# V of both mixers in rows of tokens, with V groups and gates between mixer A's q-and-k jobs

## The chip, the cores and the metric

The kernel runs on one core of a Trainium2 chip. The core's engines each work through their own instructions in order: PE (TensorE) multiplies matrices and transposes, DVE (VectorE), ACT (ScalarE) and POOL (GpSimd) work on elements, and SP issues transfers between the core's memory and the chip's. PE's sums and transposes land in eight banks of PSUM, from where DVE or ACT takes them; a bank can be used again when what stood in it has been read. The metric is the device time of one execution in microseconds (us). Before the change it is 1679.69 us, the median of three runs (1675.78 to 1680.08).

## The reference

One layer for 1024 tokens of a prompt and 32 new ones (1056 in all), model width 1024. All projections read the normed input; mixer A picks keys by an index score and a top-k, mixer B is stick-breaking attention; both have 8 heads of 64.

```
def project_inputs(x, pos, g_mix, w_in, g_qn, g_kn):
    h = rmsnorm(x, g_mix)
    z = jnp.einsum('bld,de->ble', h, w_in)
    q_a, k_a, v_a, q_i, k_i, w_i, q_b, k_b, v_b, gate_a, gate_b = jnp.split(z, SPLIT_OFFSETS, axis=-1)
    q_a = rope(rmsnorm(q_a.reshape(B, L, N_HEADS_A, HEAD_DIM), g_qn), pos)
    k_a = rope(rmsnorm(k_a.reshape(B, L, N_HEADS_A, HEAD_DIM), g_kn), pos)
    v_a = v_a.reshape(B, L, N_HEADS_A, HEAD_DIM)
    ...
    v_b = v_b.reshape(B, L, N_HEADS_B, HEAD_DIM)
...
    h = x + W_out( sigmoid(g_A) * (o_A @ W_bA) + sigmoid(g_B) * (o_B @ W_bB) )
    y = h + W_down( relu(W_up rmsnorm(h))^2 )
```

The change concerns `v_a` and `v_b`, both 1056 x 512: they are outputs of the layer, and the attention reads them again.

## The kernel before, in words

The tokens are nine tiles: 0 to 7 of 128, and tile 8, `NEW`, of 32. The model width is eight blocks k of 128. Every fp32 matrix is held as a high part and a low part (`xh`, `xl` of the input; `wh`, `wl` of the weights), and each product is three matmuls: high x high, high x low, low x high.

`unit` loads 128 x 512 weights into `wst` (three places), lets ACT cast the high part `wh`, and lets POOL (later in the kernel also DVE) subtract to get `wl`; five places (`WB`) hold `wh` and `wl`. `early` calls `unit` ahead of a job. Two kinds of jobs use the units:

- `column_block`: 128 columns of weights stand still in PE, tokens move past in chunks of 512, 272 and 272, and the sum has the output's columns in its partitions. Gates, q and k of mixer B and V use it.
- `token_rows`: a tile of 128 tokens stands still and the weights move, so the sum has tokens in its partitions. q and k of mixer A use it (256 columns a job). For `NEW`, the high and low part stand still together in 64 rows, and `join` adds the lower 32 rows to the upper by a copy on ACT and an add on DVE.

`project_v` of before is a `column_block` of two units for each of four pairs of heads (p): DVE scales the sum into `vt`, `vt` goes out as a row block of a transposed V, PE transposes it tile by tile into banks `t`, ACT casts the high part into `vs`, DVE subtracts the low part, and both go to `dv` for the attention.

The stages around the change, in the order of `run`: index scores; `project_b` for p = 0 to 3 (q and k of B, then V of B for the same p); `top_k_begin` and `top_k`, a search of 31 halvings for the top-k bound, whose counting passes (`junk`) run on ACT and DVE beside PE, followed by pieces per tile (`sgn`, `sq`, `pen`, `pre`, `mask`) that settle ties; two gates; `rope_tables`; `project_a` for p = 0 to 3 (V of A for that p, then q and k of A in nine tiles, here qk0 to qk3); two gates; then the attention reads q, k and v back. In `project_a` a tile's sum is squared by ACT (`sq`), summed (`ss`), multiplied by the tables (`ta`, `tb`) on DVE and added on POOL into `qk`; after nine tiles come the factors, the scaling of k, the transposes of `qk` into banks `t`, and the split into `az`, which goes to `dq` and `dk`. `sq`, `ta` and `tb` have one place each.

No line of the kernel is run in the order in which it is written: a recording planner (class `Plan`) takes all instructions with their rank and puts each engine's in an order by ranks and estimated times, before the program is built. The lower rank goes first: FAST 0 (emptying of a bank), PREP 1 (units), MAIN 2 (all that isn't given another, `token_rows` among it), FILL 3 (`column_block`), SLOW 4 (the search). On the chip each engine keeps that order. The banks: two `pj`, three `s`, two `t`, one `o`.

All engine instructions are issued by one helper, so the profile shows them all as line 440 (441 in the changed kernel); they are told apart by the names of their tiles.

Of the kernel before, what the change touches and what calls it, by code (L numbers as in the profile page):

```python
# [22 lines left out]
KB = D // 128  # L23
# [27 lines left out]
PACE = 16  # L51
PA_BANKS = ('s', 'pj', 's', 's', 'pj')
# [407 lines left out]
class Layer:  # L460
# [103 lines left out]
    def run(self):  # L564
# [74 lines left out]
        for p in range(2, 4):  # L639
            self.project_b(p)  # L640
            with nc.behind():
                old, new = a["ck" + "ba"[p - 2]], self.dc[H * (3 - p):H * (4 - p)]
                nc.sync.dma_start(*(z.rearrange("j e t -> (j e) t") for z in (new, old)))
        with nc.rank(SLOW):
            self.top_k_begin()
        gates = iter([*range(KB, 2 * KB), *range(KB)])
        for _ in range(2):
            self.gate(next(gates), "zb")
        self.early(*(a["w_va"][0, j] for j in range(2)), *(a["w_qka"][0, j] for j in range(3)))
# [3 lines left out]
        for p in range(4):  # L653
            self.project_a(p)
        with nc.rank(SLOW):
            self.top_k()
        for _ in range(GATES_BEFORE - 2):
            self.gate(next(gates))
# [435 lines left out]
    def project_v(self, p, mixer, w, vout):  # L1094

        nc, pr = self.nc, self.pr
        units = [self.unit(w[p, j]) for j in range(2)]
        vt = nc.tile(pr, [128, T], F32, "vt", bufs=1)

        def done(c, cs, ps):  # L1100
            nc.vector.tensor_mul(vt[:, cs], ps, self.rb[:, cs])

        self.column_block(units, self.x_of, done, self.parts)
        nc.sync.dma_start(vout[p * 128:p * 128 + 128], vt)
        for sl in GROUPS:
            pt = self.bank("t")
            m = rows(sl[0])
            nt = len(sl)
            for i, s in enumerate(sl):
                nc.tensor.transpose(pt[:m, i * 128:i * 128 + 128], vt[:, 128 * s:128 * s + m], self.ident)  # L1110
            vs = nc.tile(pr, [128, 2, 4, 128], F32R, "vs", bufs=1)
            pv = pt.rearrange("p (t h e) -> p h t e", t=4, h=2)
            for h in range(2):
                vh = vs[:m, h, :nt, 0:HD]
                nc.scalar.copy(vh, pv[:m, h, :nt])
                nc.vector.tensor_sub(vs[:m, h, :nt, HD:], pv[:m, h, :nt], vh.bitcast(F32))
            for h in range(2):
                nc.sync.dma_start(self.dv[mixer * H + 2 * p + h, :m, sl[0]:sl[0] + nt], vs.bitcast(F32)[:m, h, :nt])
# [804 lines left out]
```

## Time and profile before

| what | value |
| --- | --- |
| median of three runs | 1679.69 us |
| profiled execution, its own time | 1679.89 us |
| its span, first to last instruction | 1678.1 us |
| V of mixer B on PE, p = 0 / 1 / 2 / 3, from | 104 / 160 / 201 / 237 us |
| gates ahead of mixer A, from | 249 us |
| q-and-k jobs qk0 / qk1 / qk2 / qk3, from | 272 / 312 / 353 / 395 us |
| gates behind, first matmul of the attention | 433, 468 us |
| counting passes of the top-k search | 176 to 340 us |

The span is what the profile covers; 1.8 us of the execution lie around it. The starts are those of the first matmul of each job in PE's timeline. "PE busy" counts matmuls from start to modelled end, and they overlap; so the rate of PE is read from the distance between starts.

### The profile page before, as it was taken

How to read it: one execution, taken by the hardware profiler on the slowest of the kernel's cores; microseconds unless marked ns; L12 is line 12 of the kernel's file. 1: busy time of each engine (PE TensorE's matmuls, PEld its weight loads, DVE VectorE, ACT ScalarE, POOL GpSimd, SP SyncE). 2: the span in 40 equal slices, each digit the busy share in tenths (PEclk: the TensorE clock that was granted, in tenths of full speed). 3: DMA queues.
4: the chain of work that ended last, by engine and by line, in shares of the span. 5: the costliest groups of instructions: out<-in, count | busy, mean ns of one | idle time of the engine just before them, and what ended most of it. 6: DMA issues, size and time to landing. Idle time of an engine off the chain costs nothing.

```text
span 1678.1 us, 34748 instructions
## 1 busy us (share of the span) xinstructions
PE 1663.3 (99%) x12244; PEld 1587.8 (95%) x12244; DVE 1355.1 (81%) x2830; ACT 945.1 (56%) x2008; POOL 804.2 (48%) x681
## 2 busy tenths in 40 slices
PE   9999999999999999999999999999999999999999
PEld 9898999899989999998989999999999999999999
DVE  6777899987579889887877649998988997678775
ACT  7556888764366768886665545333333453443431
POOL 4532332344356576354556348544433466345564
PEclk9999999999999999999999999999999999999999
DMA  8243454355573636788764644444444596676674
GB/s 284 61 125 107 142 185 144 99 155 148 163 218 103 181 100 178 190 264 247 227 188 142 178 123 134 157 146 142 142 142 135 198 326 223 204 232 200 222 227 137
DMA packets 182126, 290.31 MB, mean 173 GB/s; under 512 B 29472, under 2 KB 61696, under 8 KB 181920
## 3 DMA queue, kind: packets, MB, share of 16 engines
q1 hardware_dynamic: 181664, 287.91, 55.1%
q8 instruction: 97, 1.59, 0.4%
q14 instruction: 77, 0.63, 0.1%
q10 hardware_dynamic: 288, 0.17, 0.0%
HBM read 195.09 MB, written 94.90 MB: 173 GB/s over the span
## 4 chain that ended last, share of the span: by engine, by line
PE 84%; DVE 7%; DMA 4%; ACT 2%; issue 2%; POOL 1%; SPq 1%; DVEq 0%; ACTq 0%; POOLq 0%
PE pj L440 34%; PE c L440 11%; PE a L440 11%; PE b L440 11%; PE s L440 9%; PE o L440 4%; PE t L440 4%; DVE junk L440 2%; DMA xt<-x 1%; SPq L440 1%; DVE qi L440 0%; DVE y L440 0%; DMA q<-dq 0%; DMA kl<-dc 0%; DVE ta L440 0%
## 5 line engine op out<-in xcount | busy, mean ns | idle before, releaser
L440 PE MATMUL pj<-xl,wh 128*128 128x272 f32 (+2 forms) x1200 | 334.0, 312 | 0.0
L440 POOL TENSOR_TENSOR wl<-wst,wh 128x512 fp32r<-128x512 f32 x125 | 175.4, 1408 | 219.4 <-ACT wh L440 192.9
L440 PE MATMUL pj<-xh,wh 128*128 128x272 f32 (+1 forms) x768 | 251.7, 328 | 0.0
L440 PE MATMUL pj<-xh,wl 128*128 128x272 f32 (+1 forms) x768 | 250.6, 326 | 0.2 <-POOL wl L440 0.2
L440 PEld LDWEIGHTS pj<-xl,wh 128*128 128x128 f32 x1200 | 212.7, 188 | 10.0
L440 ACT CAST wh<-wst 128x512 fp32r<-128x512 f32 x197 | 120.7, 619 | 126.6 <-PE pj L440 35.0
L440 PEld LDWEIGHTS pj<-xh,wl 128*128 128x128 f32 x768 | 144.6, 188 | 10.8 <-POOL wl L440 0.5
L440 PEld LDWEIGHTS pj<-xh,wh 128*128 128x128 f32 x768 | 144.6, 188 | 10.1 <-DVE gz L440 0.3
L440 POOL TENSOR_TENSOR p<-p,rem 128x383 f32<-128x383 f32 (+8 forms) x66 | 107.2, 1639 | 64.7 <-DVE rem L440 31.1
L440 ACT CAST wh<-us 128x512 fp32r<-128x512 f32 x80 | 49.7, 621 | 122.6 <-PE pj L440 34.3
L440 DVE TENSOR_TENSOR tt<-t,tt 128x512 fp32r<-128x512 f32 (+2 forms) x168 | 100.2, 620 | 16.8 <-ACT tt L440 16.0
L440 DVE TENSOR_TENSOR_SCAN rem<-rem,first 128x384 f32<-128x384 f32 (+8 forms) x66 | 107.2, 1642 | 2.0 <-ACT rem L440 1.6
L440 POOL TENSOR_TENSOR wl<-y,wh 128x512 fp32r<-128x512 f32 x46 | 68.6, 1492 | 77.7 <-ACT wh L440 74.7
L440 ACT ACTIVATE junk<-score,cand 128x1024 bf16<-128x1024 f32 (+2 forms) x93 | 96.9, 1042 | 12.5 <-DVE cand L440 11.0
L440 ACT CAST wh<-y 128x512 fp32r<-128x512 f32 x79 | 49.0, 621 | 96.8 <-PE c L440 20.5
L440 ACT CAST tt<-t 128x512 fp32r<-128x512 f32 (+2 forms) x168 | 85.8, 540 | 27.5 <-PE t L440 18.5
L440 PE MATMUL o<-tt,v 128*128 128x256 f32 (+1 forms) x640 | 98.5, 279 | 0.5 <-DVE o L440 0.5
L440 PE MATMUL s<-k,q 128*128 128x512 f32 (+4 forms) x384 | 98.2, 351 | 0.7 <-DMA q<-dq 0.7
L440 PEld LDWEIGHTS o<-tt,v 128*128 128x128 f32 x640 | 90.5, 189 | 6.1 <-DVE o L440 1.1
L440 DVE TENSOR_SCALAR_CACHE_REDUCE junk<-score,cand 128x384 bf16<-128x384 f32 (+1 forms) x124 | 92.9, 749 | 3.1
L440 PE MATMUL t<-ident,p 128*128 128x128 f32 (+1 forms) x596 | 90.7, 275 | 0.0
L440 POOL TENSOR_SCALAR p<-p,nb 128x384 f32<-128x384 f32 (+6 forms) x66 | 53.5, 817 | 70.8 <-DVE nb L440 59.6
(401 smaller groups left out, 5624.3 us busy)
## 6 DMA issues: line engine op xcount, KB each, us to landing
us<-w_down SPq DMA_DIRECT2D x80, 256.0 KB, 3.3
q<-dq SPq DMA_DIRECT2D x64, 256.0 KB, 4.1
du<-us SPq DMA_DIRECT2D x56, 264.0 KB, 2.7
du<-y SPq DMA_DIRECT2D x56, 264.0 KB, 3.0
y<-w_up SPq DMA_DIRECT2D x44, 256.0 KB, 2.8
k<-dk SPq DMA_DIRECT2D x40, 256.0 KB, 4.1
v<-dv SPq DMA_DIRECT2D x40, 256.0 KB, 4.0
xl<-du SPq DMA_DIRECT2D x35, 264.0 KB, 4.7
```

What stands on the lines that cost most here:

```text
L440: fn(*args, **kw)
```

## The change

- **V in rows of tokens.** `project_v` now lets a tile of tokens stand still and moves 512 columns of weights, all eight heads, past it. It works in two groups (tiles 0 to 3, tiles 4 to 8), each of which goes through all eight blocks k and holds one bank for each tile (`V_BANKS`: pj, s, pj, s, s). Each group loads its eight units anew: 16 for each mixer where there were 8. A sum is emptied by ACT, which scales it into `vz` (two places), ACT casts `vs` (two places), DVE or POOL, whichever the planner finds free, subtracts, and `vz` goes out as rows of V, `vs` to `dv`. The transposes, `vt` and the multiplication by `rb` are gone. The matmuls keep rank FILL.
- **Places.** V of B stands once, behind all four `project_b`. One gate precedes mixer A. Group 0 of V of A comes ahead of qk0, group 1 ahead of qk1, a gate ahead of qk2 and of qk3, and one gate last.
- **More places.** `qk` has two, `az` four. `early` loads five units of V of A.
- On the host the layout of `w_va`, `w_vb` is changed, and the V outputs need no transposition.

```diff
+V_BANKS = ('pj', 's', 'pj', 's', 's')
...
+        self.project_v(1, a["w_vb"], self.o["v_b"])
         with nc.rank(SLOW):
             self.top_k_begin()
         gates = iter([*range(KB, 2 * KB), *range(KB)])
-        for _ in range(2):
-            self.gate(next(gates), "zb")
-        self.early(*(a["w_va"][0, j] for j in range(2)), *(a["w_qka"][0, j] for j in range(3)))
+        self.gate(next(gates), "zb")
+        self.early(*(a["w_va"][k] for k in range(WB)))
         nc.close(self.pr, self.ik)
         self.pr = nc.open("proja")
         self.rope_tables()
         for p in range(4):
+            if p < 2:
+                self.project_v(0, a["w_va"], self.o["v_a"], (p,))
+            else:
+                self.gate(next(gates))
             self.project_a(p)
+        for _ in range(GATES_BEFORE - 3):
+            self.gate(next(gates))
         with nc.rank(SLOW):
             self.top_k()
-        for _ in range(GATES_BEFORE - 2):
-            self.gate(next(gates))
...
-    def project_v(self, p, mixer, w, vout):
+    def project_v(self, mixer, w, vout, groups=(0, 1)):
...
+        mm = nc.tensor.matmul
+        for tiles in (SUMS[g] for g in groups):
+            banks = [self.bank(V_BANKS[i]) for i in range(len(tiles))]
+            for k in range(KB):
+                wh, wl = self.unit(w[k])
+                with nc.rank(FILL):
+                    for s, ps in zip(tiles, banks):
+                        first, last = k == 0, k == KB - 1
+                        if s == NEW:
+                            x = self.xh[1][:, k, SEQ - W1:]
+                            mm(ps[:2 * DEC], x, wh, start=first, stop=False)
+                            mm(ps[:2 * DEC], x, wl, start=False, stop=last)
+                            continue
+                        xh, xl = self.x_of(k, slice(128 * s, 128 * s + 128))
+                        mm(ps, xh, wh, start=first, stop=False)
+                        mm(ps, xh, wl, start=False, stop=False)
+                        mm(ps, xl, wh, start=False, stop=last)
+            for s, ps in zip(tiles, banks):
+                m = rows(s)
+                with nc.rank(FAST):
+                    if s == NEW:
+                        self.join(ps, nc.tile(pr, [128, 512], F32, "vz", bufs=2)[:DEC])
+                    z = nc.tile(pr, [128, 512], F32, "vz", bufs=2)
+                    nc.scalar.activation(z[:m], ps[:m], AF.Copy, scale=self.rs[:m, s:s + 1])
+                    vs = nc.tile(pr, [128, H, 128], F32R, "vs", bufs=2)
+                    zv = z.rearrange("p (h e) -> p h e", h=H)
+                    nc.scalar.copy(vs[:m, :, 0:HD], zv[:m])
+                nc.either.tensor_sub(vs[:m, :, HD:], zv[:m], vs.bitcast(F32)[:m, :, 0:HD])
+                nc.sync.dma_start(vout[128 * s:128 * s + m], z[:m])
+                nc.sync.dma_start(
+                    self.dv[mixer * H:mixer * H + H, :m, s].rearrange("g p e -> p g e"), vs.bitcast(F32)[:m])
...
-        self.project_v(p, 1, a["w_vb"], self.o["v_b"])
...
-        self.project_v(p, 0, a["w_va"], self.o["v_a"])
...
-        qk = nc.tile(pr, [128, NT, 4, HD], F32, "qk", bufs=1)
+        qk = nc.tile(pr, [128, NT, 4, HD], F32, "qk", bufs=2)
...
-                zz = nc.tile(pr, [128, 2, 512], F32R, "az", bufs=2)
+                zz = nc.tile(pr, [128, 2, 512], F32R, "az", bufs=4)
```

How the planner's order moves, at three places. **PE in qk1.** Before, tiles 0 to 3 of qk1 (banks s_3930, pj_3934, s_3938, s_3942) begin beside the end of a V column block, with a transpose of the job before (qk) and four of V (vt) between their matmuls:

```order
L440 MATMUL pj_3934<-wh3_3926,xh0_104 128x256
L440 MATMUL s_3938<-wh3_3926,xh0_104 128x256
L440 MATMUL s_3942<-wh3_3926,xh0_104 128x256
L440 MATMUL t_3898<-ident_91,qk_3845 128x32
L440 MATMUL pj_3946<-wh0_3917,xh1_106 128x256
L440 MATMUL s_3930<-wl3_3927,xh0_104 128x256
L440 MATMUL s_3930<-wh3_3926,xl0_105 128x256
L440 MATMUL s_3930<-wh3_3926,xh0_104 128x256
L440 MATMUL s_3930<-wl3_3927,xh0_104 128x256
L440 MATMUL s_3930<-wh3_3926,xl0_105 128x256
L440 MATMUL t_3910<-ident_91,vt_3906 128x128 x4
```

Now tile 7 of qk1 ends (s_3729), three transposes of qk follow, then the last matmul of V's group 1, tile NEW (s_3651), and tile 3 of qk1 (s_3713), which is given the same bank:

```order
L441 MATMUL s_3729<-wh1_3697,xh1_106 128x256
L441 MATMUL s_3729<-wl1_3698,xh1_106 128x256
L441 MATMUL s_3729<-wh1_3697,xl1_107 128x256
L441 MATMUL t_3742<-ident_91,qk_3699 128x128 x3
L441 MATMUL s_3651<-wl2_3675,xh1_106 64x512
L441 MATMUL s_3713<-wh3_3688,xh0_104 128x256
L441 MATMUL s_3713<-wl3_3689,xh0_104 128x256
L441 MATMUL s_3713<-wh3_3688,xl0_105 128x256
L441 MATMUL s_3713<-wh3_3688,xh0_104 128x256
L441 MATMUL s_3713<-wl3_3689,xh0_104 128x256
```

What moved: tile 3 of qk1 stands behind the last piece of V, with no other matmul between the two users of the bank.

**DVE at the same time**, at the end of the search. Before, the first tie piece (pre_4157, for tile 2 of the masks) stands among the tables and sums of qk1's tiles:

```order
L440 ISA pen_4153,lowa_4152<-pen_4153,score7_1273 128x1024
L440 ISA lowa_4152 128x1
L440 TENSOR_REDUCE ss_3929<-sq_3943 128x4
L440 TENSOR_TENSOR ta_3944<-s_3942,tabc_3827 128x256
L440 TENSOR_TENSOR tb_3945<-s_3942,tabs_3828 128x256
L440 SCALAR_TENSOR_TENSOR pre_4157<-sq_4156,minus_4149 128x384
L440 TENSOR_REDUCE ss_3929<-sq_3947 128x4
L440 TENSOR_SCALAR needa_4154<-pre_4157,cnta1_1467 128x1
L440 TENSOR_SCALAR tfb_4167<-small_1463 128x3
L440 SCALAR_TENSOR_TENSOR pre_4157<-pre_4157,needa_4154,sgn_4155 128x384
L440 TENSOR_TENSOR ta_3948<-pj_3946,tabc_3827 128x256
L440 TENSOR_TENSOR vs_3913<-t_3912,vs_3913 128x4x64 x2
```

Now the add that `join` needs for V's tile NEW (s_3651) stands behind the pieces pen and pre of the search:

```order
L441 TENSOR_SCALAR pen_3928<-score7_1241,tfa_3926 128x1024
L441 ISA pen_3928,lowa_3927<-pen_3928,score7_1241 128x1024
L441 ISA lowa_3927 128x1
L441 TENSOR_TENSOR small_1475<-cntb0_1482,small_1475 128x3
L441 COPY_PREDICATED small_1475<-small_1475,cand_1766 128x3
L441 TENSOR_SCALAR tfb_3942<-small_1475 128x3
L441 COPY lowb_3943<-tfb_3942 32x1
L441 SCALAR_TENSOR_TENSOR pre_3932<-sq_3931,minus_3924 128x384
L441 TENSOR_SCALAR needa_3929<-pre_3932,cnta1_1479 128x1
L441 SCALAR_TENSOR_TENSOR pre_3932<-pre_3932,needa_3929,sgn_3930 128x384
L441 TENSOR_TENSOR s_3651<-s_3651,vz_3684 32x512
L441 TENSOR_TENSOR vs_3686<-vz_3685,vs_3686 32x8x64
```

What moved: an instruction that empties the bank for qk1's tile 3 comes directly behind the first tie piece, with the tables of that tile (ta_3715) only after the next one.

**PE between the two V groups of mixer B.** Before, V of B is a column block for each p (here p = 3), whose transposes (vt) stand among the block's own matmuls:

```order
L440 MATMUL pj_1455<-xh1_106,wl2_1452 128x272
L440 MATMUL pj_1455<-xh1_106,wh2_1451 128x272
L440 MATMUL pj_1455<-xl1_107,wh2_1451 128x272
L440 MATMUL t_1457<-ident_91,vt_1453 128x128 x4
L440 MATMUL pj_1455<-xh1_106,wl2_1452 128x272
L440 MATMUL pj_1455<-xh1_106,wh2_1451 128x272
L440 MATMUL pj_1455<-xl1_107,wh2_1451 128x272
```

Now the last block k of group 0 (banks pj_1399 to s_1402) is followed at once by the first of group 1, whose bank pj_1435 is that of pj_1399 and s_1438 that of s_1400:

```order
L441 MATMUL pj_1401<-wh2_1425,xl0_105 128x512
L441 MATMUL s_1402<-wh2_1425,xh0_104 128x512
L441 MATMUL s_1402<-wl2_1426,xh0_104 128x512
L441 MATMUL s_1402<-wh2_1425,xl0_105 128x512
L441 MATMUL s_1436<-wh3_1441,xh1_106 128x512
L441 MATMUL pj_1435<-wh3_1441,xh1_106 128x512
L441 MATMUL pj_1435<-wl3_1442,xh1_106 128x512
L441 MATMUL pj_1435<-wh3_1441,xl1_107 128x512
L441 MATMUL s_1436<-wl3_1442,xh1_106 128x512
L441 MATMUL s_1436<-wh3_1441,xl1_107 128x512
L441 MATMUL s_1438<-wh3_1441,xh1_106 128x512
L441 MATMUL s_1438<-wl3_1442,xh1_106 128x512
```

What moved: four banks end within twelve matmuls, and the next group begins on the free bank s_1436 and on that of pj_1399.

More of the change, by code (lines that the diff above doesn't have):

```diff
@@ L1092, in rope_tables @@
                 S.rearrange("p t (s e) -> p t s e", s=2), gx)
-    def project_v(self, p, mixer, w, vout):
+    def project_v(self, mixer, w, vout, groups=(0, 1)):
         nc, pr = self.nc, self.pr
[L1097 to L1118, printed above, removed]
@@ L1859, in _host_arrays @@
         qi[:, 256:].reshape(4, 2, 128, NI_B).transpose(0, 2, 1, 3).reshape(4, 128, 512))
-    out["w_qb"], out["w_kb"], out["w_vb"], out["w_va"] = units(qb), units(kb), units(vb), units(va)
+    out["w_qb"], out["w_kb"] = units(qb), units(kb)
+    out["w_vb"], out["w_va"] = (np.ascontiguousarray(z).reshape(KB, 128, 512) for z in (vb, va))
     out["w_g"] = units(np.concatenate([ga, gb], axis=1))
@@ L1887, in _host_arrays @@
     return out
-_OUTS = {"yT": (128, KB, T), "k_a": (T, 512), "v_a": (512, T), "k_idx": (T, HD), "k_b": (512, T), "v_b": (512, T)}
+_OUTS = {"yT": (128, KB, T), "k_a": (T, 512), "v_a": (T, 512), "k_idx": (T, HD), "k_b": (512, T), "v_b": (T, 512)}
 def _build(nc, arrays):
@@ L1917 @@
     kap, kas = pair(r["k_a"].reshape(T, H, HD))
-    vap, vas = pair(np.ascontiguousarray(r["v_a"].T).reshape(T, H, HD))
+    vap, vas = pair(r["v_a"].reshape(T, H, HD))
     kip, kis = pair(r["k_idx"])
     kbp, kbs = pair(np.ascontiguousarray(r["k_b"].T).reshape(T, H, HD))
-    vbp, vbs = pair(np.ascontiguousarray(r["v_b"].T).reshape(T, H, HD))
+    vbp, vbs = pair(r["v_b"].reshape(T, H, HD))
     return tuple(np.ascontiguousarray(z) for z in (yp, ys, kap, vap, kip, kbp, vbp, kas, vas, kis, kbs, vbs))
```

## The prediction

> **What bounds the kernel now.** I read the page first: its busy shares, its slices, its chain.
>
> ```profile
> span 1678.1 us, 34748 instructions
> PE 1663.3 (99%) x12244; PEld 1587.8 (95%) x12244; DVE 1355.1 (81%) x2830; ACT 945.1 (56%) x2008; POOL 804.2 (48%) x681
> PE 84%; DVE 7%; DMA 4%; ACT 2%; issue 2%; POOL 1%; SPq 1%; DVEq 0%; ACTq 0%; POOLq 0%
> ```
>
> TensorE (PE) is busy 99% of the span and makes 84% of the chain. So the time is what PE has to stream, plus its gaps. The change lies between about 104 us (V of mixer B) and 474 us (start of attention), so next come stretches of it: from and to, length, then busy time and instructions of PE, of its weight loads, of DVE, ACT and POOL, the clock granted, DMA.
>
> ```profile
> 82.00:200.00 118.00, 118.00 (x722) 106.25 (x723) 89.48 (x200) 78.61 (x169) 34.26 (x36) 1.00 0.41 118
> 200.00:280.00 80.00, 80.00 (x520) 73.43 (x519) 74.35 (x270) 71.42 (x141) 25.51 (x25) 1.00 0.56 179
> 280.00:475.00 195.00, 191.63 (x1407) 179.70 (x1405) 149.04 (x405) 109.73 (x238) 74.48 (x73) 1.00 0.51 146
> ```
>
> The clock is full (1.00) in all three. Up to 280 us PE has no gap: there only fewer columns help. From 280 to 475 us, mixer A's stage, 3.4 us are idle. And from 200 to 280 us DVE (93%) and ACT (89%) are nearly full as well, with the top-k search; that is the danger. What PE waits for, between 90 and 480 us:
>
> ```profile
> PE t L440 <- DVE az L440: 1.1, 1, 1.1
> PE s L440 <- DMA q<-dq: 0.7, 1, 0.7
> PE s L440 <- ACT wh L440: 0.4, 1, 0.4
> PE s L440 <- ACT sq L440: 0.4, 1, 0.4
> PE pj L440 <- POOL wl L440: 0.2, 1, 0.2
> PE s L440 <- DVE tb L440: 0.2, 1, 0.2
> PE t L440 <- DVE small L440: 0.2, 1, 0.2
> PE s L440 <- DVE cand L440: 0.2, 1, 0.2
> ```
>
> Eight waits, none repeated: 3.4 us, of which 0.7 belongs to the start of attention.
>
> **Term 1, PE's work on V: -3.9 us.** Matmuls overlap, so the price of one is the distance to the next start, not its duration. Starts in PE's timeline:
>
> ```profile
> 312.36 0.39 PE L440 MATMUL pj<-xh,wl 128*128 128x512 f32 x1
> ...
> 313.52 0.39 PE L440 MATMUL pj<-xl,wh 128*128 128x512 f32 x1
> ...
> 331.96 0.29 PE L440 MATMUL pj<-xh,wl 128*128 128x272 f32 x1
> ...
> 333.21 0.28 PE L440 MATMUL s<-wh,xh 128*128 128x256 f32 x1
> ...
> 337.10 0.28 PE L440 MATMUL s<-wl,xh 128*128 128x256 f32 x1
> ...
> 338.99 0.28 PE L440 MATMUL pj<-wl,xh 128*128 128x256 f32 x1
> ...
> 113.85 0.60 PE L440 MATMUL t<-ident,vt 128*128 128x128 f32 x4
> 114.20 0.39 PE L440 MATMUL s<-kih,qi 128*128 128x320 f32 x1
> 114.44 0.31 PE L440 MATMUL s<-kil,qi 128*128 128x320 f32 x1
> ...
> L440 PE MATMUL s<-wl,xh 128*64 128x256 f32 x32 | 7.7, 280 | 0.0
> ```
>
> From 312.36 to 313.52 are five steps of 512 columns, 0.232 us each; from 331.96 to 333.21 ten of 272, 0.125 each; from 337.10 to 338.99 sixteen of 256, 0.118 each. Four V transposes take 0.35 us, and the matmul behind them takes 0.24 where 320 columns (0.232 x 320/512) would be about 0.15; so 0.35 + 0.09 = 0.44 for four, 0.11 for one.
>
> Both mixers together lose 192 matmuls of 512 columns (44.5), 384 of 272 (48.0) and 72 transposes (7.9): 100.4 us. They gain 384 of 512 columns and 32 with 64 rows and 512 columns. The 64-row matmuls of q and k (last row) last 0.28 us, as the 128-row ones of 256 columns do, so rows cost nothing and the new shape is taken as 0.232 too. 416 x 0.232 = 96.5. Difference -3.9 us, half in B's stage, half in A's. PE is the bound in both, so it counts in full.
>
> **Term 2, waits of A's stage that go: -4 us (0 to -4.5).** The largest of them:
>
> ```profile
> 333.45 0.40 PE L440 MATMUL s<-wh,xh 128*128 128x256 f32 x2
> 334.91 0.24 PE L440 MATMUL t<-ident,qk 32*128 32x32 f32 x1 [1.06 <-DVE az L440]
> ```
>
> By starts this is 1.46 less two steps of 0.118, 1.22 us where the view says 1.06: 0.16 more. The seven waits that aren't attention's sum to 2.7; with 0.16 each, 3.8; a few shorter gaps without a named wait make about 4. With V in rows there are no vt tiles, no V transposes and no second user of the t banks; with two qk tiles and four az tiles a q-and-k job needn't wait for the job before. All of these waits stand at places that the new order doesn't have, so I take them as gone, and count what the new order has instead in terms 3 and 4. Bound 0: each is replaced by one as long.
>
> **Term 3, a new wait in qk1: +4 us (2.3 to 9).** In the new order the last matmul of V's second group (tile NEW, bank s_3651) stands directly ahead of tile 3 of qk1, s_3713, which takes the same bank: V's matmuls have rank FILL, qk1's rank MAIN, so qk1 ran past V's end. PE is in order, so at s_3713 everything behind it waits until the bank is free: matmul end, ACT copies the lower half, DVE adds it, ACT scales the sum out. Matmul tail 0.4, copy 0.6 (the row of p<-s below), add 0.7, scaling 0.6: 2.3 us if both engines come at once. But ahead of the add, DVE has the search's pen, ISA, pre, needa, pre, and these need the end of the search on ACT. When does PE come there, and when ACT?
>
> PE: from the last common place, 113.95 us, the order holds 624 matmuls of 512 columns, 392 of 256, 337 of 272, 28 of 384 and 320, 21 transposes: 144.8 + 46.3 + 42.1 + 4.6 + 2.4 = 240.2, so 354.1, with an earlier gap or two 355.
>
> ACT, between the search's start and its end:
>
> ```profile
> L440 ACT ACTIVATE junk<-score,cand 128x1024 bf16<-128x1024 f32 (+2 forms) x93 | 96.9, 1042 | 12.5 <-DVE cand L440 11.0
> L440 ACT CAST vs<-t 128x256 fp32r<-128x256 f32 (+1 forms) x24 | 6.3, 312 | 0.2 <-PE t L440 0.2
> L440 ACT CAST zz<-zb 128x272 fp32r<-128x272 f32 (+1 forms) x12 | 5.7, 475 | 2.9 <-DVE zb L440 2.9
> ...
> 176.00:341.00 165.00, 162.84 (x1112) 150.70 (x1111) 153.54 (x548) 141.12 (x281) 58.62 (x58) 1.00 0.49 150
> ...
> L440 ACT ACTIVATE p<-s 128x512 f32<-128x512 f32 x39 | 23.8, 614 | 5.0 <-PE s L440 3.3 <-PE t L440 1.7
> ```
>
> In the new order that stretch of ACT holds 17 more casts of weights, 16 scalings and 16 casts of V, all of 512 columns and taken by the row of p<-s: 49 x 0.614 = 30.1; the 24 casts vs<-t go (6.3), and six zz casts and three sigmoids fall outside (about 4): +20 us. All groups of the stretch sum to 159 us where ACT was busy 141.12, since neighbours overlap; so 0.89 of it, +17.7. The search ended, by these rows, at its first sgn:
>
> ```profile
> 340.63 0.62 ACT L440 ACTIVATE sgn<-score,lowa 128x384 bf16<-128x384 f32 x1
> ...
> 340.84 1.07 DVE L440 TENSOR_SCALAR pen<-score,tfa 128x1024 f32<-128x1024 f32 x1
> 343.05 1.58 DVE L440 CUSTOM_DVE_ANT_0 pen<-pen,score 128x1024 f32<-128x1024 f32 x1
> 345.56 0.94 DVE L440 TENSOR_TENSOR_SCAN pre<-sq,minus 128x384 f32<-128x384 bf16 x1
> 346.97 0.62 DVE L440 SCALAR_TENSOR_TENSOR pre<-pre,needa,sgn 128x384 f32<-128x384 f32 x1
> ```
>
> So sgn comes at 358.3 if ACT's idle time stays, and at 347.3 if the 11.0 us that it waited for DVE's cand are used. DVE becomes lighter, which speaks for the second; I take the middle, 353. From sgn to the free bank: pen (from 0.2 after it) 1.07, ISA 1.58, pre 0.94, needa 0.2, pre 0.62, add 0.7, scaling 0.6, less some overlap: about 5.5. 353 + 5.5 - 355 = 3.5, and 4 with half of a search pass (junk, 1.0) that may run ahead; by 347.3 the floor, 2.3; by 358.3 it is 9.
>
> A later end of the search costs nothing behind it, since the last of its masks was there 70 us before attention:
>
> ```profile
> L440 ACT ACTIVATE mask<-sq x7: 508/740/1057, 348.9 to 402.7; 128x384 bf16<-128x384 bf16 x1, 128x512 bf16<-128x512 bf16 x1, 128x640 bf16<-128x640 bf16 x1, 128x1024 bf16<-128x1024 bf16 x1
> ```
>
> DVE's part, from the tiles of V and of the weights' low parts:
>
> ```profile
> L440 DVE TENSOR_TENSOR vt<-pj,rb x24: 423/442/692, 112.4 to 415.2; 128x272 f32<-128x272 f32 x16, 128x512 f32<-128x512 f32 x8
> L440 DVE TENSOR_TENSOR vs<-t,vs x48: 201/413/425, 115.2 to 433.9; 128x256 fp32r<-128x256 f32 x32, 32x64 fp32r<-32x64 f32 x16
> ...
> L440 DVE TENSOR_TENSOR wl<-wst,wh x72: 674/693/1811, 471.4 to 1645.8; 128x512 fp32r<-128x512 f32 x72
> ```
>
> Ahead of the search's end 15 vt (10 x 0.44 + 5 x 0.69 = 7.9) and 28 vs (18 x 0.41 + 10 x 0.2 = 9.4) go, and ten subtractions of 512 columns come, 0.69 each by the median of wl: 6.9. DVE is lighter by some 10 us.
>
> That median has a maximum of 1.81 beside it, while vs<-t,vs never passed 0.425. [...]
>
> **Term 4, other new waits: +4 us (1 to 8).** Behind tile 3, in the same order: tile NEW of qk1 takes the bank of s_3713 at once (sq, ta, tb behind the next search piece on DVE: 1.2 to 2.2 us), and the gate's third block stands at once behind its first, whose bank it takes (matmul tail and DVE's gz of 0.7: about 1.2). At the four changes between V groups ACT must empty a bank in 2.3 to 2.8 us, with the third eviction behind the store of the first (vz has two places): 0 to 1 each. In sum 4. Sixteen more units of weights cost nothing on PE: a group takes one in 12 x 0.232 = 2.8 us, ACT's cast of one takes 0.6, and POOL, which makes the low part, was busy 25.51 of the 80 us from 200 on; without that cover each microsecond of delay would be one of PE.
>
> **Term 5, the start of attention: 0 (-1 to +1).** q<-dq cost 0.7 and can move either way. From there on the same instructions run, and from the FFN on in the same order.
>
> Sum: -3.9 - 4 + 4 + 4 = 0.1 us. The profiled execution took 1679.89 us (span 1678.1 and 1.8 around it), 0.2 over the median shown: **1680 us**.
>
> **Rivals.** *Faster*: the search ends by 350, the bank in qk1 costs 2.3, the rest 1, the old waits go in full, attention gains 1: -3.9 - 4.5 + 2.3 + 1 - 1 = -6.1, 1673.8. For it: DVE's relief and the 11.0 us idle on cand. Against: ACT's load. Chance 0.22. *Slower*: ACT keeps its idle time, the search ends at 358, and since V's last bank hangs on it, PE waits 9 in qk1 and 6 elsewhere: -3.9 - 4 + 15 = +7, 1687. It decides from an sgn later than about 356.5. For it: ACT at 89% already. Chance 0.16. *Subtractions stretched* from 0.69 to 1.81 (the row of wl): ten of them take back the 10 us of DVE's relief, half of it lands on the search, 5 us more in qk1: 1685. Chance 0.07; POOL was busy only 58.62 of 165 us, so most would meet it idle. [...] *The new places don't matter*: term 2 is 0, and so are half of terms 3 and 4: -3.9 + 4 = 0, the same time by another way, 0.1. My forecast as worked out, 0.45.
>
> **The numbers.** A measurement of this kernel tells about 0.3%, 5 us, from no change. Faster by more: the first rival, 0.22. Slower by more: second and third, 0.23. Within: 0.55. The outer sums are 1673.8 and, with terms 3 and 4 at their tops and term 2 at 0, 1693; leaving the thin ends off, 1673.5 to 1688.
>
> **What would show it.** PE's matmul starts between 104 and 250 us without gaps, and V's stretch shorter by 2 us there; a wait of PE's s for ACT vz (or DVE s) near 355 us, 2.3 to 9 long, on the first matmul of qk1's tile 3; the first sgn at 347 to 358; no wait for az or for q<-dq of az. I am wrong if the search moves past 360, if V groups wait for wl, or if that one wait isn't there.

## The result: 1694.9 us, about 1% slower

The changed kernel takes 1694.91 us (median of five runs, 1693.38 to 1698.88) where the kernel before takes 1679.69 in the runs beside it. The ratio is 1.0102, with a 95% interval of 1.0087 to 1.0117. The prediction was 1680, with a range of 1673.5 to 1688. The profiled execution took 1693.38 us (span 1691.6).

The same views of the changed kernel's profile as before. First the page (busy time, share, instructions), then three stretches of the span (length, busy time of PE, of its weight loads, of DVE, ACT and POOL, the clock, DMA):

```profile
PE 1661.3 (98%) x12012; PEld 1573.0 (93%) x12012; DVE 1349.3 (80%) x2773; ACT 973.7 (58%) x2022; POOL 816.8 (48%) x702
...
82.00:200.00 118.00, 118.00 (x716) 106.06 (x716) 86.96 (x190) 78.47 (x162) 42.10 (x45) 1.00 0.46 127
200.00:280.00 80.00, 78.11 (x359) 63.02 (x358) 65.19 (x223) 74.17 (x137) 35.39 (x32) 1.00 0.62 194
280.00:490.00 210.00, 196.20 (x1367) 179.89 (x1366) 159.33 (x410) 135.87 (x266) 89.71 (x85) 0.99 0.52 152
```

PE is 2 us less busy in a span that is 13.5 us longer, so it is idle for 15.5 us more. Some 10 of these lie in the last row: 13.8 us, where before had 3.4 in its own stretch of that stage. What PE waited for from 90 to 490 us (total, times, longest):

```profile
PE s L441 <- ACT vz L441: 4.0, 1, 4.0
PE s L441 <- DMA q<-dq: 2.8, 2, 1.8
PE pj L441 <- ACT wh L441: 2.5, 2, 1.7
PE pj L441 <- DVE gz L441: 1.7, 1, 1.7
PE s L441 <- DVE tb L441: 1.4, 1, 1.4
PE pj L441 <- DVE tb L441: 1.3, 2, 0.7
PE t L441 <- DVE az L441: 1.0, 1, 1.0
PE t L441 <- POOL qk L441: 0.8, 1, 0.8
PE pj L441 <- POOL wl L441: 0.2, 1, 0.2
```

15.7 us in twelve waits, 3.4 in eight before. The first is the one that term 3 forecast. By the starts in PE's timeline the stages compare so (us; "first gate" is the first matmul of the first gate, "fifth gate" that of the gate behind mixer A's stage, "first score" and "last of attention" are the attention's first score matmul and its last matmul on V):

| | first gate | fifth gate | first score | last of attention | end of PE |
| --- | --- | --- | --- | --- | --- |
| before | 249.0 | 458.3 | 468.7 | 896.1 | 1674.5 |
| after | 246.6 | 464.6 | 478.2 | 908.6 | 1687.4 |
| longer by, in the stage | -2.4 | +8.7 | +3.2 | +3.0 | +0.4 |

One caution on the last stages. The fifth gate has 72 matmuls, and those that are left at the first score run later, between the attention's. In before 9 were left, in the changed kernel none. They are matmuls of 272 columns, 0.125 us each by term 1, so some 1.1 us (an estimate) has moved from attention to the stretch ahead of it: of the +3.2, about 2.1 is lost time, and attention lost about 4.1 and not 3.0. The rows of these stretches, before's attention first, then the changed kernel's way from the first to the fifth gate, from there to the first score, and its attention:

```profile
468.70:896.10 427.40, 425.29 (x2931) 393.02 (x2930) 354.98 (x804) 314.75 (x696) 236.84 (x194) 1.00 0.64 189
```

```profile
246.60:464.60 218.00, 205.91 (x1401) 187.30 (x1399) 175.61 (x486) 157.84 (x299) 98.61 (x94) 0.99 0.49 144
464.60:478.20 13.60, 11.85 (x73) 10.54 (x72) 2.14 (x5) 1.56 (x5) 0.00 (x0) 1.00 0.81 221
478.20:908.60 430.40, 424.50 (x2919) 391.68 (x2920) 354.82 (x806) 317.78 (x698) 221.93 (x191) 1.00 0.63 187
```

### The profile page after: what moved, and what is told of

Read it like the earlier page. It is cut to its first block, busy times and chain, and to the rows that moved or that the text cites. A ratio compares the mean times of both kernels' runs of the same rounds, so it can differ in the third digit from the quotient of the medians.

```text
span 1691.6 us, 34214 instructions
## 1 busy us (share of the span) xinstructions
PE 1661.3 (98%) x12012; PEld 1573.0 (93%) x12012; DVE 1349.3 (80%) x2773; ACT 973.7 (58%) x2022; POOL 816.8 (48%) x702
## 4 chain that ended last, share of the span: by engine, by line
PE 90%; DVE 5%; DMA 2%; issue 1%; ACT 1%; POOL 0%; SPq 0%; ACTq 0%; DVEq 0%; POOLq 0%
PE pj L441 34%; PE s L441 14%; PE c L441 11%; PE a L441 11%; PE b L441 11%; PE o L441 5%; PE t L441 4%; DMA q<-dq 1%; DVE ml L441 1%; DVE y L441 0%; DVE wl L441 0%; DVE pre L441 0%; DVE junk L441 0%; DVE qi L441 0%; SPq L441 0%
## 5 line engine op out<-in xcount | busy, mean ns | idle before, releaser
L441 POOL TENSOR_TENSOR wl<-wst,wh 128x512 fp32r<-128x512 f32 x138 | 191.1, 1391 | 197.5 <-ACT wh L441 180.5
L441 PE MATMUL pj<-xl,wh 128*128 128x272 f32 (+2 forms) x1008 | 272.7, 310 | 0.0
L441 ACT CAST wh<-wst 128x512 fp32r<-128x512 f32 x213 | 130.2, 621 | 130.2 <-PE pj L441 32.8
L441 PE MATMUL pj<-xh,wh 128*128 128x272 f32 (+1 forms) x576 | 188.3, 327 | 3.1 <-DVE gz L441 1.7
L441 PE MATMUL pj<-xh,wl 128*128 128x272 f32 (+1 forms) x576 | 187.9, 326 | 0.0
L441 PEld LDWEIGHTS pj<-xl,wh 128*128 128x128 f32 x1008 | 176.9, 188 | 8.3
L441 PEld LDWEIGHTS pj<-xh,wh 128*128 128x128 f32 x576 | 108.4, 188 | 11.7 <-DVE gz L441 2.0
L441 PEld LDWEIGHTS pj<-xh,wl 128*128 128x128 f32 x576 | 108.5, 188 | 7.6
L441 PE MATMUL s<-wh,xh 128*128 128x256 f32 (+3 forms) x312 | 96.1, 314 | 5.7 <-ACT vz L441 4.0
L441 PE MATMUL s<-wl,xh 128*128 128x256 f32 (+3 forms) x312 | 96.1, 314 | 0.0
```

Source lines behind the costliest of these rows:

```text
L441: fn(*args, **kw)
```

## The wait that was forecast, and what came behind it

The first tie piece, from the group of sgn in the changed kernel (shortest, median, longest in ns; first and last start); then ACT, DVE and PE around the bank of V's tile NEW, from the timeline:

```profile
L441 ACT ACTIVATE sgn<-score,lowa x4: 616/760/1134, 355.8 to 380.8; 128x384 bf16<-128x384 f32 x1, 128x512 bf16<-128x512 f32 x1, 128x640 bf16<-128x640 f32 x1, 128x1024 bf16<-128x1024 f32 x1
...
359.86 0.68 DVE L441 TENSOR_TENSOR s<-s,vz 32x512 f32<-32x512 f32 x1
...
361.37 0.68 ACT L441 ACTIVATE vz<-s,rs 32x512 f32<-32x512 f32 x1
...
357.58 0.48 PE L441 MATMUL s<-wl,xh 128*64 128x512 f32 x1
362.10 0.39 PE L441 MATMUL s<-wh,xh 128*128 128x256 f32 x1 [4.04 <-ACT vz L441]
```

The search ended at 355.8 (forecast 353, between 347 and 358), PE came at 358 (forecast 355), the add stood behind the tie piece, the scaling came last, and the wait was 4.04 us (forecast 4). The mechanism is right to this point. That the size is so near is in part luck: both ends came 3 us later than forecast, and the scaling began 0.8 us after the add's end, since ACT was at two search pieces (sq and sgn), which the chain of the prediction hadn't in it. What I had no term for stands in the clock of the same stretch (second number from the right but two):

```profile
362.00:363.00 1.00, 0.90 (x7) 0.90 (x8) 0.00 (x0) 1.00 (x4) 0.00 (x0) 1.00 0.07 18
363.00:364.00 1.00, 1.00 (x7) 1.00 (x6) 0.94 (x2) 0.50 (x1) 0.00 (x0) 0.53 0.20 47
364.00:365.00 1.00, 1.00 (x7) 1.00 (x6) 0.96 (x2) 0.00 (x0) 0.00 (x0) 0.50 0.29 65
365.00:366.00 1.00, 1.00 (x7) 1.00 (x7) 0.88 (x2) 0.00 (x0) 0.00 (x0) 0.50 0.31 66
366.00:367.00 1.00, 0.73 (x4) 0.53 (x3) 0.00 (x0) 0.23 (x1) 0.00 (x0) 0.76 0.00 0
```

One microsecond after PE had restarted, its clock fell to 0.50 and stayed there until about 366.5: some 3.4 us, in which a step of 256 columns took 0.214 us (thirteen steps from 363.43 to 366.21 in PE's timeline) where term 1 has 0.118. So it is up to 1.7 us more for a wait of 4 (an estimate: half of the spell; by the steps it is 1.5). So the wait cost more than its length. Before, where no wait passed 1.4 us, the clock was 1.00 from 6.2 us to the end of the span.

So where does the stage's +8.7 come from? By the prediction's own terms: V's work -2, the waits of before gone -2.7, the wait for vz 4.0, half clock 1.7, and the other waits of the stage 8.1 where I had 4 (wh 1.7, gz 1.7, tb 1.4 and 1.3, az 1.0, qk 0.8, wl 0.2): 9.1 in sum. That comes near it, but it says where PE stood, not which part of the change made it stand. The runs do.

## The experiments

Fourteen kernels, each against the kernel before on the same chip. The places of the four gates are written as ahead of mixer A / between its jobs / behind them; before is 2/0/2, the changed kernel 1/2/1. The expectations weigh three theories of the loss. Theory 1: waits that the new order makes in mixer A's stage. Theory 2: ACT can't keep up with emptying V's banks beside the search. Theory 3: the planner lays attention out anew, whatever the stage ahead does. Theories F, G and H are explained where they come.

### V of one mixer in rows, and the places

V of B alone in rows, behind all four project_b, everything else as before:

```diff
+        self.project_v(1, a["w_vb"], self.o["v_b"])
...
-        self.project_v(p, 1, a["w_vb"], self.o["v_b"])
```

> The kernel before with only V of mixer B in rows, once behind all four project_b; V of A in columns, gates and places as before. The changed kernel's first gate began 2.4 us earlier than before, so theory 1 expects that gain here as well and nothing lost in mixer A's stage beyond what before lost: 1676 to 1679. Theory 2 expects that ACT's load delays the search and so mixer A's stage: 1680 to 1685. Theory 3: plus or minus 4 by the new order in attention alone.

Measured 1682.48 us, ratio 1.0019 (1.0008 to 1.0030). The way to the fifth gate is 4.9 us shorter (453.4), better than I thought; but from the first score to the last matmul of attention it takes 433.2 us where before took 427.4. The stage isn't delayed, so theory 2 falls for B; the longer attention fits theory 3.

V of A alone in rows, V of B in columns, gates 2/0/2, places as before (`early` loads five units of V of A, as in the changed kernel):

```diff
-        self.project_v(p, 0, a["w_va"], self.o["v_a"])
...
+        if p < 2:
+            self.project_v(0, a["w_va"], self.o["v_a"], (p,))
```

> The kernel before with only V of mixer A in rows (group 0 ahead of qk0, group 1 ahead of qk1, rank FILL); V of B in columns, gates and places as before. Its order has the same pair as the changed kernel: the last V matmul of tile NEW directly ahead of the tile of qk1 that takes its bank. Theory 1: the wait of 2.3 to 5 us at that matmul is there again, with clock 0.50 behind it where it is about 4; 1684 to 1692. Theory 2: ACT is less loaded here than in the changed kernel (no V of B on it), so the wait is under 2.5 and the time 1678 to 1682.

Measured 1693.37, 1.0092 (1.0077 to 1.0107). The wait for vz is there (3.0 us, and 0.50 behind it, from 371.5 to 374.9 us), and PE waits on through qk2 and qk3 (az 3.6 in three, f 1.8, sq 1.8, tb 1.7). So 14 us can be lost, and the wait for vz can come, with no gate moved. This made me think that V of A in columns had been the work beside each q-and-k job; e5 was to test that.

The more places alone, and az alone, on the kernel before:

```diff
-        qk = nc.tile(pr, [128, NT, 4, HD], F32, "qk", bufs=1)
+        qk = nc.tile(pr, [128, NT, 4, HD], F32, "qk", bufs=2)
-                zz = nc.tile(pr, [128, 2, 512], F32R, "az", bufs=2)
+                zz = nc.tile(pr, [128, 2, 512], F32R, "az", bufs=4)
```

> The kernel before with only the two more places: qk 2, az 4. If the places take away the waits that I counted for them (az 1.1, and the idle of ACT behind dq<-az), 1 to 3 us faster than before: 1677 to 1679. If they don't matter, 1679 to 1680. If a changed order alone costs microseconds in attention, as theory 3 would have it, the start of attention or the stretch to 930 us can be up to 5 us longer: up to 1685.

> The kernel before with az 4 alone, qk left at 1: the smallest change of order before attention. Theory 3 (the planner lays attention out anew whenever the stage ahead ends differently, and the layout of before is a good one among many): attention, from its first matmul to its last, takes 429 to 434 us where before took 427.4, and the time is 1680 to 1685 though the stage ahead isn't longer. If attention only suffers from what the changed stage leaves behind (stores, late loads), it stays at 427 to 428 and the time at 1677 to 1680.

Measured 1683.01 (1.0025, 1.0016 to 1.0034) and 1681.57 (1.0013, 1.0003 to 1.0022): slower, though the fifth gate comes earlier (457.5 and 455.9 against 458.3). Attention takes 432.8 and 435.1 us. Not one of its instructions is changed; only its order is, since the stage ahead ends differently. Some 2.0 us of the longer attention is the fifth gate's: 25 of its matmuls were left at the first score, where before had 9. PE's idle time in attention's stretch, 5.2 and 7.2 us where before has 2.1, is the real loss.

### V's rank, and the changed kernel with fewer places

```diff
-                with nc.rank(FILL):
+                with nc.rank(MAIN):
```

> The changed kernel with V's matmuls given rank MAIN instead of FILL, so that qk1 can't run past the end of V's second group; the bank of V's tile NEW is then no longer taken by the very next matmul. Theory 1 (the time was lost to waits that the order makes in mixer A's stage: a late V end on a bank that qk1 needs): the 4.0 us wait of s for ACT vz at qk1 is gone, and with it the stretch of about 3 us behind it at clock 0.50; 1694.9 falls by 5 to 7, to 1688 to 1690. Theory 2 (V in rows costs because ACT, which now empties V's banks beside the search, can't keep up, wherever V's end stands): the wait only moves to another matmul; 1693 to 1697. Theory 3 (the start of attention and the order inside it lost the rest, some 7 us, whatever mixer A's stage does): those 7 stay in either case.

Measured 1691.94, 1.0086 (1.0069 to 1.0102): 3 us below the changed kernel's median, not 5 to 7, and the two intervals overlap, so the gain isn't clear of noise. The wait for vz is gone, but a wait of 2.4 us for wl stands in qk0 and one of 2.4 for az at the stage's end, with a spell of half clock (0.50 from 460.1 to 467.0 us). Theory 1 explains a part at most.

The changed kernel with `qk` 1 and `az` 2:

> The changed kernel with qk 1 and az 2 as before. I counted 4 us for waits that the places and the missing V transposes take away, and the places alone gave 0.8 us up to the gate behind mixer A's stage. If they do the same here: 1695 to 1697. If in the changed order the places let qk1 run ahead of V's end (MAIN before FILL, with a second qk to write to), fewer places would hold it back and remove the wait at tile NEW: 1687 to 1691.

Measured 1699.72, 1.0124 (1.0109 to 1.0139): 4.8 us over the changed kernel's median, 3.7 by the two ratios, with intervals that overlap. The wait for vz stays (3.9 us), and at the stage's end the transposes wait 6.3 us for az, where the changed kernel waits 1.0: in this order the places take away a wait of some 5 us.

### The gates

The changed kernel with the gates back where before has them, 2/0/2:

```diff
-        self.gate(next(gates), "zb")
+        for _ in range(2):
+            self.gate(next(gates), "zb")
...
-            else:
-                self.gate(next(gates))
...
-        for _ in range(GATES_BEFORE - 3):
+        for _ in range(GATES_BEFORE - 2):
```

> The changed kernel with the gates where the kernel before has them: two ahead of mixer A, none between its q-and-k jobs, two behind. Theory F (V of A in columns was the work that PE did beside each of the four q-and-k jobs while their sums were emptied; in two groups ahead of qk0 and qk1 it is used up by qk1, and only the gates between are left beside qk2 and qk3): without these gates qk2 and qk3 wait as they did with V of A alone (e4), and the stretch from the first gate to the gate behind the stage grows by 2 to 5 us over the changed kernel; 1695 to 1699. Rival (the gates between the jobs are what costs): 1688 to 1692.

Measured 1681.23, 1.0017 (1.0008 to 1.0026). Theory F falls: without gates between the jobs the kernel is 13.7 us faster, not slower. With all else as in the changed kernel, the gates' places make nearly the whole loss, and with them the wait for vz comes and goes: here it isn't there. PE's waits from 240 to 480 us, and the same three stretches as above:

```profile
PE s L441 <- DVE tb L441: 2.3, 1, 2.3
PE t L441 <- POOL qk L441: 1.3, 1, 1.3
PE pj L441 <- POOL wl L441: 1.2, 2, 0.9
PE s L441 <- DMA q<-dq: 0.9, 1, 0.9
PE s L441 <- ACT az L441: 0.5, 1, 0.5
PE s L441 <- DVE f L441: 0.3, 1, 0.3
```

```profile
246.70:458.20 211.50, 205.77 (x1402) 187.86 (x1401) 175.49 (x490) 149.10 (x293) 93.44 (x90) 0.98 0.53 156
458.20:466.40 8.20, 8.20 (x48) 7.12 (x47) 1.13 (x2) 1.37 (x4) 0.00 (x0) 1.00 0.72 199
466.40:897.00 430.60, 427.08 (x2952) 395.74 (x2951) 349.81 (x804) 322.39 (x701) 234.44 (x195) 1.00 0.63 187
```

Here 27 of the fifth gate's matmuls are left at the first score (3.4 us by term 1's 0.125), so the equal lengths of attention hide a gain: PE is idle for 3.5 us in it, and for 5.9 in the changed kernel.

V's groups spread over qk0 and qk2, gates ahead of qk1 and qk3, still 1/2/1:

```diff
-            if p < 2:
-                self.project_v(0, a["w_va"], self.o["v_a"], (p,))
+            if p % 2 == 0:
+                self.project_v(0, a["w_va"], self.o["v_a"], (p // 2,))
```

> The changed kernel with V's group 0 ahead of qk0 and group 1 ahead of qk2, the gates ahead of qk1 and qk3, so that FILL work is spread over all four jobs. In its order the last V matmul of tile NEW isn't followed by a user of its bank. Theory F: the wait for vz goes and the stage is 4 to 7 us shorter: 1687 to 1691. Theory 2 (ACT can't empty V's four or five banks in time, wherever they stand): same waits at another place, 1693 to 1697. In either case attention keeps the 3 to 6 us that it lost in all of the runs so far.

Measured 1692.79, 1.0083 (1.0068 to 1.0098). That is within the noise of the changed kernel. The wait for vz is gone, and others are there in its place: 2.4 for az at the stage's end, 1.7 for wh in V's first group as in the changed kernel. V's place alone doesn't make the loss.

One gate put back at each end, 1/1/2 and 2/1/1:

> The changed kernel with one gate ahead of mixer A, one between (ahead of qk2) and two behind, instead of 1, 2 and 1. Theory G (the two gates behind qk3 are the cover under which its last sums are scaled, transposed, split, stored and read back; with one gate the first k is read 8.0 us after the next gate begins instead of 2.9): with two behind, the read comes within 2 to 4 us of that gate, the waits for q<-dq at the start of attention and for az at the stage's end go, and 1694.9 falls by 4 to 8. Theory H (the missing second gate in front is what costs, since V's units then come late and V's groups meet the search): nothing of that changes, 1692 to 1696.

> The changed kernel with two gates ahead of mixer A, one between (ahead of qk2) and one behind. Theory H: the wait for wh in V's first group (1.7 us near 272) goes and V's second group ends later against the search, so the 4.0 us wait for vz goes too; 1694.9 falls by 5 to 9. Theory G: the start of attention still waits, 3 to 5 us of the loss stay; 1690 to 1695.

Measured 1686.62 (1.0044, 1.0029 to 1.0059) and 1683.58 (1.0026, 1.0015 to 1.0037). Both gain, 8.3 and 11.3 us. With two behind, the time from the fifth gate to the first score falls from 13.6 to 8.5 us, and the wait for vz (4.0) stays; with two ahead the waits for wh and vz go, the fifth gate comes 9.1 us earlier, and q<-dq is waited for 2.9 us. Against e5 (2/0/2, the same but for the gates) the gate taken from ahead costs 5.4 us here and the one taken from behind 2.4, which isn't clear of noise; the sum is less than the 13.7 of both.

The two parts that had shortened the way to attention, V of B in rows and the more places, with V of A in columns and gates 2/0/2:

> The kernel before with V of B in rows and with the two more places (qk 2, az 4), V of A in columns, gates as before: the two parts that each shortened the way to attention (4.9 and 0.8 us at the gate behind mixer A's stage). If these add up, that gate starts at 452 to 454 us instead of 458.3. For the whole: if attention loses 3 to 6 us in every order but the one of before, 1679 to 1682; if its loss was a matter of how the stage ends, 1673 to 1676.

Measured **1673.01**, ratio 0.9967 (0.9955 to 0.9978): faster than both kernels. The fifth gate comes at 452.7, and attention takes 428.9. On this version the gates can be moved with V of A in columns. First as the change moves them, 1/2/1; with it goes the place at which `top_k` is recorded, behind the last gate as in the changed kernel and in e5, where before and e8 have it ahead of the gates behind. What that is worth by itself wasn't tried.

> The version with V of B in rows, V of A in columns and more places (1673.0) with the gates moved as the changed kernel has them: one ahead, one before qk2, one before qk3, one behind. Theory G: the cover behind is lost whatever shape V of A has, so 3 to 6 us slower: 1676 to 1679. Rival (gates between the jobs only hurt together with V of A in rows): 1671 to 1674.

Measured 1693.55, 1.0088 (1.0071 to 1.0104): 20.5 us slower, more than three times what I expected, and with V of A in columns. Then one gate from ahead to behind (1/0/3) and one from behind to ahead (3/0/1), none between and `top_k` left in its place:

> The version with V of B in rows, V of A in columns and more places (1673.0, two gates ahead and two behind) with one gate ahead and three behind; no gate between. If the cover behind qk3 is what a gate is worth and the one ahead of mixer A is worth little while V of A is in columns: 1670 to 1674, the wait for q<-dq at the start of attention gone. If the gate ahead is worth as much (mixer A's q-and-k jobs begin 12 us earlier, in the middle of the search, and wait for DVE): 1677 to 1683, with the loss between the first gate and the first gate behind.

> The same version with three gates ahead of mixer A and one behind. If the cover behind qk3 matters: the last q and k come back late, a wait of 2 to 4 us for q<-dq at the first s and half clock behind it, 1677 to 1682. If only the start of mixer A against the search matters: as good as or better than two and two, 1669 to 1674.

Measured 1681.69 (1.0019, 1.0009 to 1.0028) and 1693.68 (1.0089, 1.0074 to 1.0104): 8.7 and 20.7 us slower than 2/0/2. There is no gate between the jobs here, so it isn't the gates between that cost. The gates at both ends are cover (work that PE can do while another chain isn't ready): in this version the one taken from behind costs more, in the changed kernel's version it was the one taken from ahead (e10 and e11). PE's waits from 240 to 480 us, first with 2/0/2, then 1/0/3, then 3/0/1:

```profile
PE s L441 <- ACT gz L441: 1.4, 1, 1.4
PE s L441 <- ACT wh L441: 0.5, 1, 0.5
PE s L441 <- DVE small L441: 0.3, 1, 0.3
PE t L441 <- DVE vs L441: 0.3, 1, 0.3
```

```profile
PE t L441 <- DVE vt L441: 2.9, 3, 1.4
PE pj L441 <- DVE tb L441: 1.6, 1, 1.6
PE t L441 <- DVE vs L441: 1.0, 1, 1.0
PE pj L441 <- DVE vt L441: 0.7, 1, 0.7
PE pj L441 <- DVE gz L441: 0.7, 1, 0.7
...
```

```profile
PE t L441 <- DVE az L441: 3.1, 2, 2.2
PE pj L441 <- DVE vt L441: 1.6, 1, 1.6
PE pj L441 <- DVE tb L441: 1.1, 1, 1.1
PE pj L441 <- ACT wh L441: 1.0, 1, 1.0
PE t L441 <- DVE small L441: 0.9, 1, 0.9
...
```

With one gate ahead, qk0 begins at 258 instead of 270 us, and what PE waits for is nearly all DVE (7.2 of 8.2 us). With one gate behind, PE waits most at the end of the stage, for az. How much work stands there shows in the two ways of the end: with 2/0/2, 94 gate matmuls run between the last matmul of qk3 (427.0) and the last transpose of qk (446.0), and 50 are left for the time in which dq and dk are written; with 3/0/1 there are 72, all used by then (442.4 to 460.9). The read of the first k follows late. From the group of these reads, before, changed kernel, its gates put back (e5), 2/0/2 and 3/0/1 (issue time in ns, first and last start):

```profile
L440 SPq DMA_DIRECT2D k<-dk x40: 319/428/1316, 461.2 to 851.0; - x40
```

```profile
L441 SPq DMA_DIRECT2D k<-dk x40: 319/431/1343, 472.6 to 864.0; - x40
```

```profile
L441 SPq DMA_DIRECT2D k<-dk x40: 319/424/637, 459.8 to 847.5; - x40
```

```profile
L441 SPq DMA_DIRECT2D k<-dk x40: 319/428/1756, 455.3 to 844.7; - x40
```

```profile
L441 SPq DMA_DIRECT2D k<-dk x40: 319/432/1647, 469.3 to 863.4; - x40
```

Against the fifth gate's start (458.3, 464.6, 458.2, 452.7, 461.1) the first read is issued 2.9, 8.0, 1.6, 2.6 and 8.2 us later: with one gate behind, the fifth gate is all used up, or nearly, before q and k are back. That is the q<-dq of 2.8 us in the changed kernel's waits.

What PE lost can be set side by side. Each entry is PE's idle time in a stretch (its length less PE's busy time in the profiled execution) plus half of the time in which PE ran at a granted clock of 0.50 (an estimate of what the spell cost), in us:

| version | gates | first to fifth gate | to the first score | attention |
| --- | --- | --- | --- | --- |
| before | 2/0/2 | 2.6 | 0.0 | 2.1 |
| changed kernel | 1/2/1 | 13.8 | 1.8 | 5.9 |
| e10 | 1/1/2 | 16.0 | 0.0 | 2.1 |
| e11 | 2/1/1 | 5.7 | 4.6 | 5.4 |
| e5 | 2/0/2 | 7.7 | 0.0 | 3.5 |
| e12, V of A in columns | 1/2/1 | 7.0 | 2.8 | 5.8 |
| e14, V of A in columns | 1/0/3 | 7.8 | 0.0 | 0.9 |
| e15, V of A in columns | 3/0/1 | 7.7 | 3.1 | 7.3 |
| e8, V of A in columns | 2/0/2 | 1.2 | 0.0 | 2.2 |

The column in the middle is the clearest. All seven versions with one gate behind (these four, e1, e6 and e13) lose 1.8 to 4.7 us there, and none of the nine with two or more loses anything. A missing gate ahead shows in the first column, where e15, with three ahead, loses as much, most of it at the stage's end. The attention column goes with the gate behind in these nine, but e2, e3, e4 and e9, with two behind, lose 4.5 to 8.2 us in attention, so there the order counts as well. Against its own 2/0/2 (e5 or e8), the entries of a row make up two thirds or more of the longer span; the rest shows neither as idle time nor as half clock.

## Why the prediction was wrong

The step that failed is the gates: the prediction gave their move no term. It counted V's columns, the places and the bank in qk1, and took the gates as work that only changes its place. The runs put 13.7 us on that move alone (e5), where the whole miss was 15.

The account of the change, part by part: V of B in rows with the more places -6.1 us (1673.0 against 1679.1); V of A in rows besides +8.2 (1681.2, with `top_k`'s place in it); the gates' move +13.7 (1694.9). It holds for this order of the parts. In another order they have other prices: V of A in rows costs 14.0 put on before alone (e4), and 1.4, within the noise, put on the version that has its gates moved already (e12), where the gates' move costs 20.5. The parts share what they cost.

- **Term 1, V's work -3.9**: right where it can be seen apart. Up to the first gate half of it was due, 2.0, and 2.4 came.
- **Term 2, waits that go -4**: not shown as a whole. Waits of the same kinds came at other places and are counted under term 4; one sign failed, since there was to be no wait for az, and one of 1.0 us is there at the stage's end, as long as the one of before. That the places are worth something in the new order e13 shows (3.7 to 4.8 us, at the edge of the noise). That they would make attention slower behind an otherwise unchanged stage (e2, e9) I had not in it.
- **Term 3, the new wait in qk1 +4**: 4.04 us, by the steps given, with both ends 3 us late. Left out was the half clock behind it, up to 1.7.
- **Term 4, other new waits +4**: 8.1, twice as much. The wait for wh (1.7) is in a part to which I gave nothing: "Sixteen more units of weights cost nothing on PE". It is gone with two gates ahead (e5, e11), so it isn't the units' number but how early V's first group begins.
- **Term 5, the start of attention 0 (-1 to +1)**: here the failed step shows in the prediction's own words. "q<-dq cost 0.7 and can move either way. From there on the same instructions run": it looked at what runs there and not at what had covered it. Taking a gate from behind qk3, and one from ahead of mixer A, was never priced. The way to the first score got 3.2 us longer where I had at most 1 (1.8 us of it PE stands idle), attention 3.0, and a sign failed here as well: q<-dq was waited for 2.8 us. The move of the gates as a whole cost 13.7 with V of A in rows and 20.5 with it in columns.
- **The slower rival** (the search ends late, qk1 waits 9) has the right sign and the wrong mechanism: sgn came at 355.8, before the 356.5 from which it was to decide.
- **The subtractions stretched**: the trace has them. In the changed kernel the new subtractions on DVE (shortest, median, longest in ns):

```profile
L441 DVE TENSOR_TENSOR vs<-vz,vs x11: 679/691/4787, 220.7 to 363.1; 128x512 fp32r<-128x512 f32 x10, 32x512 fp32r<-32x512 f32 x1
```

Three of the eleven are stretched, by 5.5 us in sum. The longest began at 284.06 us and took 4.79 us, while POOL ran tabs and two wl beside it, back to back, behind a wl that it had begun before. The forecast that most would meet POOL idle supposes that POOL's work is what stretches them; the prediction's row of wl doesn't show that by itself, but this trace agrees with it: the three began while POOL had an instruction running, and the other eight, none over 0.69 us, began with POOL idle. The search still ended within the forecast, at 355.8, and in e10, where no subtraction passed 1.84 us, at 356.1, with the same wait for vz of 4.04 us. So this rival didn't make the wait; what it cost elsewhere wasn't tried apart.

What stays open: attention takes 428.1 to 435.1 us in the profiles of the other versions where before takes 427.4, and up to 3.4 us of that is the fifth gate's matmuls that run in it. Less these, and before less its own 1.1, e8 is as long as before and e10 and e14 are shorter, so the layout of before isn't the best one; that a changed order can cost 3 to 6 us of idle time and half clock in attention is shown (e2, e3, e9), why it does in these and not in those isn't. And why the gate ahead is worth 8.7 us is shown only as far as that PE then waits for DVE, in the time of the search and behind it.

## What to carry to other kernels

Independent work that stands beside a chain is cover, and it has a price where it is taken from: before a filler is moved, count what waits at the place that it leaves. A chain that ends in a store and a load back (here sums, scaling, transposes, split, write, read) needs its cover behind it. Here a gate less behind cost 2.4 us in one version (e11 against e5, not clear of noise) and 20.7 in another (e15 against e8), where the change took 4 us of work from PE. And where a planner orders everything, a small edit changes the order far behind it: judge parts by runs, stage by stage, since they don't add up (+3.1 and +3.6 us alone, -6.1 together).

## What the runs showed of the hardware

The granted clock of TensorE fell to 0.50 beside waits of 4 us and beside some of under 2. In the profiles of these kernels each wait of 2.8 us or more from 240 to 480 us has a spell at 0.50 that begins within it or up to 2.2 us behind it. Of the shorter waits some have one and some don't, and here their length doesn't decide: the same wait of 1.7 us for wh, which ends near 274 us, was followed by one in e10 and e13 and not in the changed kernel and e6. The spells last 3.4 us (changed kernel, 363.1 to 366.5), about 6.8 (e1, 460.1 to 467.0) or about 10.2 (e13, 467.7 to 478.0, begun within a wait of 6.3 us that ended at 471.9): once, twice and three times 3.4. The wait of 4.04 us cost some 5.7 us in the changed kernel and some 7 in e10, where the spell went on until 368.4 us (estimates: the wait and half of the spell behind it). Why a spell follows one wait and not another isn't shown.

One subtraction on VectorE took seven times its usual time. vs (128 x 512 elements, vs<-vz,vs) lasted 0.69 us at the median and 4.79 us once (284.06 us in the changed kernel), while four instructions of GpSimd of 1.3 to 1.5 us followed one another beside it. Two more took 1.36 and 1.37 us (230.44 and 337.88). Each of the three began while GpSimd had an instruction running (wl from 229.96, wl from 283.10 and the three behind it, vs from 337.41) and ended some 0.55 us after GpSimd's end (231.25, 288.30 and 338.70). That GpSimd held them up is argued from these times alone: no run moved GpSimd's work and nothing else.
